# Small products of an RWKV-7 head pair: the odd head's results go to the other half of the rows, so that a group works in four quarters of TensorE

## The chip, the core and the metric

One core of a Trainium2 chip runs the whole program in one launch. The metric is the device time of one execution in microseconds (us). PE is TensorE, PEld its weight loads, DVE VectorE, ACT ScalarE, POOL GpSimd, SP SyncE (it issues most of the DMAs).

## What is computed

The reference is a trunk of two layers on 512 tokens of width 1024. Each layer is a half-step SwiGLU FFN, a mixing sub-layer and another FFN, each behind an RMSNorm with a shift, a scale and a gate from a condition vector. The mixing sub-layer projects the tokens to 20 tiles of 128 columns, and gives them to three kinds of heads: windowed attention (8 query heads), RWKV-7 time mixing (4 heads of 64) and a short convolution. The change is in the RWKV part only. What a head has to compute is this recurrence over the tokens:

```
def step(S, inp):
    r_t, w_t, k_t, v_t, kk_t, a_t = inp
    s_kk = einsum('bhvk,bhk->bhv', S, kk_t)
    S = S * w_t[:, :, None, :] - s_kk[..., None] * (kk_t * a_t)[:, :, None, :] + v_t[..., None] * k_t[:, :, None, :]
    return S, einsum('bhvk,bhk->bhv', S, r_t)
```

## The kernel before

The activations are kept transposed: 128 channels on the rows (partitions), 512 tokens along the columns. Large products are made in three passes of a split number format (`mm3`, lines 121 to 123: high by high, high by low, low by high), 128x128 weights by 512 columns, and each weight tile is split by ACT (`wH`, line 133) and DVE (`wL`, line 135) before use.

The recurrence is computed in chunks of 64 tokens. The function `rwkv(q)` does it for one pair of heads, q = 0 and q = 1; each layer calls it for both, so there are four calls. The two heads of a pair are e = 0 (channel rows 0 to 63) and e = 1 (rows 64 to 127), and the 8 chunks are numbered by block b (0 to 3) and half c (0 and 1): chunk n = 2b + c. In the tiles of a pair, chunk halves c lie on the rows, `rows[c]`, and e and b along the columns. The steps, with the names that the profile shows:

- `pairs` (L811) makes `B` (from `be`, the tile that was `a`) and `K` (from `ka`, the tile that was `iP`): products into two PSUM tiles `ps_c`, one for each e, then one masked copy for each by DVE (L814). The matrix to be inverted is `LT`, a part of `B`.
- The 16x16 blocks of its diagonal are inverted by DVE, after a detour by DRAM (`elim`, `inv`, L839 and L840). The result, `C`, becomes the tile `T` and by a transpose `TT` (L888, L889).
- `ps_xv` (L874): `K` times the values, copied by ACT to a half of `AX` (L875).
- Two levels that put the blocks together: `X` = mask of `LT` by `T` (products `ps_x`, DVE L902), `T` minus `TT` by `X` (products `ps_t`, L906, at level 0 only), and `TT` minus `X` by `TT` (products `ps_tt`, L909).
- `W` = minus `TT` by `AX` (products `ps_w2`, which the profile calls `ps_w`, L916; ACT L917, one copy for each e).
- `ps_gn` (L926 to L933), `ps_o` (L942 to L949), then the six serial steps over the chunks (`ps_s`, L954), `ps_ys`, the group norm (`ps_m`, `ps_v`, a reciprocal at L972, L973 and L974) and the gate (`ps_g`).

All of these are 64x64 or 64x128 products, 64 rows deep. Which quarter of TensorE's 128x128 array a product takes follows from where its operands' rows and its result's rows lie. In `ps_xv`, `ps_x`, `ps_t`, `ps_tt` and `ps_w2` the result stands on the same rows as the operands, so that only two of the four quarters are used:

```
def each(name, lhs, rhs):
    pt = psum([P, 2, NB, CH], name, R)
    for e in range(2):
        for b in range(NB):
            for c in range(2):
                mm(pt[rows[c], e, b], lhs[rows[c], e, b], rhs[rows[c], e, b], start=True, stop=True)
    return pt
```

In `ps_c`, `ps_gn` and `ps_o` the operands lie on the rows of one of c and e, the results on the rows of the other: four quarters. Each head pair has one PSUM tag (`R` is r0 or r1) with two buffers.

The order of the work is set in two stages. `rwkv` and `attention` are generators; each `yield` names a cost in us, and the loop at the end of `mix` puts steps of the projection (`products`, one step is three large products) between them, in proportion to that cost: RWKV_WORK and ATT_WORK are the sums of the yields, FILL_WORK the projection work there is to share out. After that a scheduler orders the instructions of each engine by what it expects to be ready, so that products of one group can be put between those of another. On the chip each engine then works off its list in order.

Of the kernel before, what the change touches and what calls it, by code (L numbers as in the profile page):

```python
# [12 lines left out]
ALU = mybir.AluOpType  # L13
# [4 lines left out]
P = 128  # L18
# [8 lines left out]
NB = T // P  # L27
CH = 64
# [3 lines left out]
PAD = 24  # L32
GAP = 448
GROUPS = ((0, 12), (12, 22))
RWKV_WORK, ATT_WORK, FILL_WORK = 29.8, 15.2, 129.6


def _columns(spec):
# [20 lines left out]
def trunk_kernel(ctx, tc, ins, out, layers=L, phases=("ffn1", "mix", "ffn2")):  # L59
    nc = tc.nc  # L60
# [14 lines left out]
    tt, stt, ts = nc.vector.tensor_tensor, nc.vector.scalar_tensor_tensor, nc.vector.tensor_scalar  # L75
    act, mm = nc.scalar.activation, nc.tensor.matmul
# [7 lines left out]
    def psum(shape, name, tag="x"):  # L84
        return ps.tile(shape, F32, name=name, tag=tag, bufs=2)

    def psmm(tags=("mm",)):
        turn[0] += 1
        return psum([P, T], "ps_mm", tags[turn[0] % len(tags)])
# [49 lines left out]
    rows = (slice(0, CH), slice(CH, P))  # L139
# [33 lines left out]
    def cst(name):  # L173
        a, b = CON[name]
        return con[:, a:b]

    def rep(name, n):
        a = cst(name)
        return a.unsqueeze(1).to_broadcast([P, n, a.shape[1]])

    def rep2(name, n):
        a = cst(name)
        return a.unsqueeze(1).unsqueeze(1).to_broadcast([P, 2, n, a.shape[1]])
# [100 lines left out]
    def load_w(src, n=KD, raw=None, pair=None, behind=None):  # L284

        w = raw or wp.tile([P, KD, P], F32, name="wraw", tag="wraw", bufs=2)
        wH, wL = pair or (wp.tile([P, KD, P], F32R, name=x, tag=x, bufs=4) for x in ("wH", "wL"))
        loads.append(nc.sync.dma_start(w[:, :n], src))
        split(wH[:, :n], wL[:, :n], w[:, :n], behind)
        return wH, wL  # L290
# [292 lines left out]
    def mix(l, hn, ss, mp, then, ready):  # L583
# [5 lines left out]
        def pair(name):  # L589
            pool = hnp[name in ("y4", "y5", "yr")]  # L590
            return tuple(pool.tile([P, T], F32R, name=name + n, tag="hn") for n in "HL")

        def S(q, name, shape=(P, T)):
            return mp.tile(list(shape), F32, name=f"{name}{q}", tag=f"s{q}", bufs=8)

        def U(q, name, shape):
            return mp.tile(shape, F32, name=f"{name}{q}", tag=f"u{q}", bufs=4)
# [147 lines left out]
        def rwkv(q):  # L745

            R = f"r{q}"
# [56 lines left out]
            def pairs(src, name):  # L804
                M = U(q, name, [P, 2, NB, 2, CH])
                pts = [psum([P, NB, 2, CH], "ps_c", R) for _ in range(2)]
                for b in range(NB):
                    for c in range(2):
                        n = 2 * b + c
                        for e in range(2):  # L810
                            mm(pts[e][rows[c], b], src[rows[e], n * CH : (n + 1) * CH], AR[rows[e], :, n], start=True, stop=True)  # L811
                msk = con[:, CON["su"][0] : CON["iu"][1]].unsqueeze(1).to_broadcast([P, NB, 2 * CH])
                for e in range(2):
                    tt(M[:, e].rearrange("p b a t -> p b (a t)"), pts[e].rearrange("p b a t -> p b (a t)"), msk, ALU.mult)  # L814
                yield 1.4
                return M

            B_ = yield from pairs(be, "B")
            LT = B_[:, :, :, 0]

# [6 lines left out]
            for c in range(2):  # L827
                for m in range(NM):
                    n = (c * NM + m) * 2 * NB
# [6 lines left out]
            for s in range(BASE - 1):  # L836
                n = BASE - 1 - s
# [10 lines left out]
            AX = U(q, "AX", [P, 2, NB, 2, CH])  # L848
# [7 lines left out]
            def tcopy(src, name):  # L856
                t = blocks(S(q, name))
                nc.scalar.copy(t, tmajor(src, "ps_" + name))
                return t

            def alphas():
                pt = tmajor(AR[:, 0].rearrange("p c t -> p (c t)"), "ps_ta")
                for e in range(2):
                    nc.scalar.copy(AX[:, e, :, 0], pt[:, :, rows[e]])


            K_ = yield from pairs(ka, "K")
            vN = tcopy(v_[q], "vN")
            yield 0.4
            px = psum([P, 2, NB, CH], "ps_xv", R)  # L870
            for e in range(2):
                for b in range(NB):
                    for c in range(2):
                        mm(px[rows[c], e, b], K_[rows[c], e, b, 0], vN[rows[c], b, rows[e]], start=True, stop=True)  # L874
            nc.scalar.copy(AX[:, :, :, 1], px)  # L875
            yield 1.3
            alphas()
            yield 0.4
            beN = tcopy(be, "beN")
# [4 lines left out]
            T_ = S(q, "T", (P, 2, NB, CH))  # L884
            TT = S(q, "TT", (P, 2, NB, CH))
# [3 lines left out]
            nc.vector.transpose(TT.rearrange("p e b t -> p (e b t)"), T_.rearrange("p e b t -> p (e b t)"))  # L889
            X = S(q, "X", (P, 2, NB, CH))  # L890

            def each(name, lhs, rhs):
                pt = psum([P, 2, NB, CH], name, R)
                for e in range(2):
                    for b in range(NB):
                        for c in range(2):
                            mm(pt[rows[c], e, b], lhs[rows[c], e, b], rhs[rows[c], e, b], start=True, stop=True)
                return pt

            for lev in range(2):  # L900
                px = each("ps_x", LT, T_)
                tt(X, px, rep2(f"lev{lev}", NB), ALU.mult)  # L902
                yield 1.3
                if lev == 0:
                    p1 = each("ps_t", TT, X)
                    tt(T_, T_, p1, ALU.subtract)  # L906
                    yield 1.3
                p2 = each("ps_tt", X, TT)
                tt(TT, TT, p2, ALU.subtract)  # L909
                yield 1.3  # L910
            Wn = AX.rearrange("p e b a t -> p e b (a t)")
            for e in range(2):
                pt = psum([P, NB, P], "ps_w2", R)
                for b in range(NB):
                    for c in range(2):
                        mm(pt[rows[c], b], TT[rows[c], e, b], Wn[rows[c], e, b], start=True, stop=True)  # L916
                nc.scalar.mul(Wn[:, e], pt, -1.0)  # L917
                yield 1.1

            GT = chunks(S(q, "GT"))  # L920
            N = chunks(S(q, "N"))
            pgs = [psum([P, 2, NB, CH], "ps_gn", R) for _ in range(2)]
            ce = [(c, e) for c in range(2) for e in range(2)]
            for b in range(NB):
                for c, e in ce:
                    mm(pgs[c][rows[e], 0, b], Wn[rows[c], e, b, :CH], beN[rows[c], b, rows[e]], start=True, stop=True)  # L926
# [13 lines left out]
            for b in range(NB):  # L940
# [4 lines left out]
                for c, e in ce:  # L945
                    mm(pos[c][rows[e], 1, b], vN[rows[c], b, rows[e]], K_[rows[c], e, b, 1], start=False, stop=True)
            for c, po in enumerate(pos):
# [3 lines left out]
            for c in range(1, NC - 1):  # L951
                pt = psum([P, CH], "ps_s", R)
# [4 lines left out]
            pt = psum([P, NC, CH], "ps_ys", R)  # L957
# [107 lines left out]

        prod = products()
        live, waiting = {}, {"rwkv0": lambda: rwkv(0), "rwkv1": lambda: rwkv(1), "att": attention}
        left, fill, credit = 2 * RWKV_WORK + ATT_WORK, FILL_WORK, 0.0
        more = True
# [28 lines left out]
        for q in range(2):  # L1098
            x = pair("yr")
# [3 lines left out]
        for n in range(2):  # L1103
            w = load_w(wo2[l, n], 6)
            for d in range(3):
                i = 3 * n + d
                pt = psmm(BANKS[1:3])
# [10 lines left out]
        for i, w, _ in got["last"]:  # L1118
            pt = psmm(BANKS[1:3])[:, : T // 2]
# [140 lines left out]
    for n, (l, p) in enumerate(seq):  # L1260
# [3 lines left out]
        if n + 1 < len(seq):  # L1264
            l1, p1 = seq[n + 1]
# [15 lines left out]
        else:  # L1281
            w, need = ("w1", (l, 7)) if p == "ffn1" else ("w2", (l + 1, 1))
# [88 lines left out]
```

## Time and profile before

| | us |
|---|---|
| median of 3 runs | 1867.47 (1863.78 to 1871.3) |
| the profiled execution, its time | 1866.04 |
| its span | 1864.0 |
| PE busy | 1828.7 (98%) |
| DVE busy | 1398.4 (75%) |
| ACT busy | 836.3 (45%) |

Engines' busy times overlap; PE's are partly modelled, since matmuls are pipelined. In the rows of the profile an fp32 product shows as two records. The groups of the change lie between 465 and 568 us in layer 0, and between 1378 and 1482 us in layer 1.

### The profile page before, as it was taken

The numbers are of one execution on the slowest core, as the hardware profiler recorded it, in microseconds if no ns is written. First come the engines' busy times: TensorE is split into PE (matmuls) and PEld (weight loads), VectorE is DVE, ScalarE is ACT, GpSimd is POOL, SyncE is SP. The second block draws the span as 40 slices with busy tenths as digits, with TensorE's granted clock in tenths as the row PEclk, the third lists the DMA queues.
The fourth block names the chain that finished last, engine by engine and source line by source line (L and its number), as shares of the span: only waits on it lengthen the run. The fifth ranks groups of instructions, "written<-read, shape, count | busy, mean of one in ns | idle before, by whom it ended". The sixth has DMA issues, their size and how long they took to land.

```text
span 1864.0 us, 33421 instructions
## 1 busy us (share of the span) xinstructions
PE 1828.7 (98%) x13664; PEld 1644.4 (88%) x13664; DVE 1398.4 (75%) x2202; ACT 836.3 (45%) x1272; POOL 130.9 (7%) x212
## 2 busy tenths in 40 slices
PE   8999999999999999999999999999999999999999
PEld 6889899986777999899999988999767788998998
DVE  7687677867986887777878786777589778874872
ACT  4443255346422555245345524544563335532551
POOL 0101110100000000110100020110000000100100
PEclk8999999999999999999999999999999999999999
DMA  7667876621122475886737688773212125775752
GB/s 307 225 185 234 263 197 202 221 83 46 58 55 72 136 195 176 296 223 195 246 112 197 171 272 228 192 229 114 101 56 59 53 68 161 209 227 139 203 144 68
DMA packets 104313, 308.24 MB, mean 165 GB/s; under 512 B 23392, under 2 KB 24416, under 8 KB 103136
## 3 DMA queue, kind: packets, MB, share of 16 engines
q1 hardware_dynamic: 75936, 203.34, 32.3%
q0 software_dynamic: 28224, 102.77, 21.7%
q8 instruction: 107, 1.75, 0.4%
q14 instruction: 46, 0.38, 0.1%
HBM read 302.66 MB, written 3.41 MB: 164 GB/s over the span
## 4 chain that ended last, share of the span: by engine, by line
PE 71%; DVE 13%; DMA 7%; issue 4%; ACT 4%; POOL 1%; SPq 0%; POOLq 0%; DVEq 0%; ACTq 0%
PE ps_mm L121 11%; PE ps_mm L122 10%; PE ps_mm L123 10%; PE ps_d L420 6%; PE ps_d L422 6%; PE ps_d L421 6%; PE ps_f L420 3%; PE ps_f L422 3%; PE ps_f L421 3%; DMA wada<-in_wadaT 2%; DVE wL L135 2%; PE ps_g L422 2%; PE ps_g L420 2%; PE ps_g L421 2%; ACT wH L133 1%
## 5 line engine op out<-in xcount | busy, mean ns | idle before, releaser
L133 ACT CAST wH<-wraw 128x1024 fp32r<-128x1024 f32 (+2 forms) x292 | 266.1, 918 | 434.7 <-PE ps_mm L122 190.2
L135 DVE TENSOR_TENSOR wL<-wraw,wH 128x1024 fp32r<-128x1024 f32 (+2 forms) x292 | 307.2, 1058 | 105.1 <-ACT wH L133 104.4
L123 PE MATMUL ps_mm<-actH,wL 128*128 128x512 f32 (+1 forms) x784 | 281.5, 359 | 2.8 <-DVE wL L135 2.8
L121 PE MATMUL ps_mm<-actH,wH 128*128 128x512 f32 (+1 forms) x784 | 281.6, 359 | 0.0
L122 PE MATMUL ps_mm<-actL,wH 128*128 128x512 f32 (+1 forms) x784 | 281.2, 359 | 0.0
L121 PE MATMUL ps_mm<-hnH,wH 128*128 128x512 f32 (+1 forms) x760 | 267.5, 359 | 5.7 <-ACT hnH L133 2.9
L122 PE MATMUL ps_mm<-hnL,wH 128*128 128x512 f32 (+1 forms) x760 | 266.5, 353 | 0.5
L123 PE MATMUL ps_mm<-hnH,wL 128*128 128x512 f32 (+1 forms) x760 | 266.4, 353 | 0.6 <-DVE wL L135 0.6
L420 PE MATMUL ps_d<-comH,wH 128*128 128x256 f32 x816 | 224.7, 275 | 0.3 <-ACT s L446 0.3
L421 PE MATMUL ps_d<-comL,wH 128*128 128x256 f32 x816 | 224.4, 275 | 0.0
L422 PE MATMUL ps_d<-comH,wL 128*128 128x256 f32 x816 | 224.4, 275 | 0.0
L192 DVE SCALAR_TENSOR_TENSOR wada<-wada,crep 128x1024 f32<-128x1024 f32 x140 | 167.7, 1219 | 48.8 <-DMA wada<-in_wadaT 48.2
L135 DVE TENSOR_TENSOR wL<-sum,wH 128x1024 fp32r<-128x1024 f32 x102 | 124.9, 1224 | 71.5 <-ACT wH L133 71.3
L123 PEld LDWEIGHTS ps_mm<-actH,wL 128*128 128x128 f32 x784 | 149.1, 190 | 20.3 <-DVE wL L135 3.6
L121 PEld LDWEIGHTS ps_mm<-hnH,wH 128*128 128x128 f32 x760 | 143.4, 191 | 24.9 <-issue 3.8
L121 PEld LDWEIGHTS ps_mm<-actH,wH 128*128 128x128 f32 x784 | 149.1, 190 | 16.8
L122 PEld LDWEIGHTS ps_mm<-actL,wH 128*128 128x128 f32 x784 | 149.0, 190 | 16.8
L123 PEld LDWEIGHTS ps_mm<-hnH,wL 128*128 128x128 f32 x760 | 145.5, 191 | 19.3 <-issue 4.3
L122 PEld LDWEIGHTS ps_mm<-hnL,wH 128*128 128x128 f32 x760 | 145.4, 192 | 17.2 <-DVE hnL L277 1.6
L420 PEld LDWEIGHTS ps_d<-comH,wH 128*128 128x128 f32 x816 | 156.7, 192 | 0.9 <-ACT s L446 0.9
L422 PEld LDWEIGHTS ps_d<-comH,wL 128*128 128x128 f32 x816 | 156.7, 192 | 0.0
L421 PEld LDWEIGHTS ps_d<-comL,wH 128*128 128x128 f32 x816 | 156.7, 192 | 0.0
(354 smaller groups left out, 3855.6 us busy)
## 6 DMA issues: line engine op xcount, KB each, us to landing
wada<-in_wadaT POOLq DMA_DIRECT2D x128, 512.0 KB, 4.8
wraw<-in_wmi SPq DMA_DIRECT2D x40, 512.0 KB
wraw<-in_w2p SPq DMA_DIRECT2D x36, 512.0 KB
wraw<-in_w1p SPq DMA_DIRECT2D x32, 512.0 KB
wraw<-in_w1o SPq DMA_DIRECT2D x32, 384.0 KB
wraw<-in_w2o SPq DMA_DIRECT2D x32, 384.0 KB
wraw<-in_w1i SPq DMA_DIRECT2D x20, 512.0 KB
wraw<-in_w1o SPq DMA_DIRECT2D x32, 320.0 KB
```

Source lines behind the costliest of these rows:

```text
L121: mm(acc, wH, xH, start=start, stop=False)
L122: mm(acc, wH, xL, start=False, stop=False)
L123: mm(acc, wL, xH, start=False, stop=stop)
L133: nc.scalar.copy(hi, src)
L135: return nc.vector.tensor_sub(lo, src, hi.bitcast(F32))
L192: stt(w, w, 1.0, crep, ALU.mult, ALU.mult, accum_out=out_)
L420: mm(acc, wH, xH, start=start and i + k == 0, stop=False, skip_group_check=True)
L421: mm(acc, wH, xL, start=False, stop=False, skip_group_check=True)
L422: mm(acc, wL, xH, start=False, stop=k == 3, skip_group_check=True)
```

## The change

The products of `ps_xv`, `each` and `ps_w2` put the odd head's (e = 1) results on the other half of the rows, `rows[c ^ e]`. The four combinations of e and c then lie in the four quarters of the array, and each group is issued in the order `corners`. For it each group gets two PSUM tiles, one for each e (`quarters`), and takes both buffers of its tag. The result is then read in three pieces (`gathered`): the even head as a whole, 128 rows, and the odd head as two halves of 64 rows which change places. At level 0 both products, the one for `T` and the one for `TT`, are put into one pair of tiles under the name `ps_t` (it was `ps_t` and `ps_tt`), and the yield between them goes. `W` is made for both heads at once. In `pairs`, `ps_gn` and `ps_o` the loops over e and c run backwards. The yields get other costs, and RWKV_WORK, their sum, falls from 29.8 to 25.7.

```diff
-RWKV_WORK, ATT_WORK, FILL_WORK = 29.8, 15.2, 129.6
+RWKV_WORK, ATT_WORK, FILL_WORK = 25.7, 15.2, 129.6
...
                     for c in range(2):
                         n = 2 * b + c
-                        for e in range(2):
+                        for e in (1, 0):
                             mm(pts[e][rows[c], b], src[rows[e], n * CH : (n + 1) * CH], AR[rows[e], :, n], start=True, stop=True)
...
+            corners = [(b, e, c) for b in range(NB) for e, c in ((1, 1), (1, 0), (0, 1), (0, 0))]
+
+            def quarters(name, n=1, w=CH):
+                return [psum([P, n, NB, w], name, R) for _ in range(2)]
+
+            def gathered(pts, j):
+                return [(slice(0, P), 0, pts[0][:, j])] + [(rows[c], 1, pts[1][rows[1 - c], j]) for c in range(2)]
...
-            px = psum([P, 2, NB, CH], "ps_xv", R)
-            for e in range(2):
-                for b in range(NB):
-                    for c in range(2):
-                        mm(px[rows[c], e, b], K_[rows[c], e, b, 0], vN[rows[c], b, rows[e]], start=True, stop=True)
-            nc.scalar.copy(AX[:, :, :, 1], px)
-            yield 1.3
+            pts = quarters("ps_xv")
+            for b, e, c in corners:
+                mm(pts[e][rows[c ^ e], 0, b], K_[rows[c], e, b, 0], vN[rows[c], b, rows[e]], start=True, stop=True)
+            for r, e, x in gathered(pts, 0):
+                nc.scalar.copy(AX[r, e, :, 1], x)
+            yield 0.8
...
+            def each(pts, j, lhs, rhs):
+                for b, e, c in corners:
+                    mm(pts[e][rows[c ^ e], j, b], lhs[rows[c], e, b], rhs[rows[c], e, b], start=True, stop=True)
 
             for lev in range(2):
-                px = each("ps_x", LT, T_)
-                tt(X, px, rep2(f"lev{lev}", NB), ALU.mult)
-                yield 1.3
+                pts = quarters("ps_x")
+                each(pts, 0, LT, T_)
+                for r, e, x in gathered(pts, 0):
+                    tt(X[r, e], x, rep(f"lev{lev}", NB)[r], ALU.mult)
+                yield 0.8
+                pts = quarters("ps_t", 2 - lev)
                 if lev == 0:
-                    p1 = each("ps_t", TT, X)
-                    tt(T_, T_, p1, ALU.subtract)
-                    yield 1.3
-                p2 = each("ps_tt", X, TT)
-                tt(TT, TT, p2, ALU.subtract)
-                yield 1.3
+                    each(pts, 1, TT, X)
+                each(pts, 0, X, TT)
+                for j, to in ((1, T_), (0, TT))[lev:]:
+                    for r, e, x in gathered(pts, j):
+                        tt(to[r, e], to[r, e], x, ALU.subtract)
+                yield 1.4 - 0.6 * lev
...
-            for e in range(2):
-                pt = psum([P, NB, P], "ps_w2", R)
-                for b in range(NB):
-                    for c in range(2):
-                        mm(pt[rows[c], b], TT[rows[c], e, b], Wn[rows[c], e, b], start=True, stop=True)
-                nc.scalar.mul(Wn[:, e], pt, -1.0)
-                yield 1.1
+            pts = quarters("ps_w2", 1, P)
+            for b, e, c in corners:
+                mm(pts[e][rows[c ^ e], 0, b], TT[rows[c], e, b], Wn[rows[c], e, b], start=True, stop=True)
+            for r, e, x in gathered(pts, 0):
+                nc.scalar.mul(Wn[r, e], x, -1.0)
+            yield 1.3
...
-            ce = [(c, e) for c in range(2) for e in range(2)]
+            ce = [(c, e) for c in (1, 0) for e in (1, 0)]
```

More of the change, by code (lines that the diff above doesn't have):

```diff
@@ L890, in rwkv @@
             X = S(q, "X", (P, 2, NB, CH))
-            def each(name, lhs, rhs):
-                pt = psum([P, 2, NB, CH], name, R)
-                for e in range(2):
-                    for b in range(NB):
-                        for c in range(2):
-                            mm(pt[rows[c], e, b], lhs[rows[c], e, b], rhs[rows[c], e, b], start=True, stop=True)
-                return pt
-            for lev in range(2):
-                px = each("ps_x", LT, T_)
-                tt(X, px, rep2(f"lev{lev}", NB), ALU.mult)
-                yield 1.3
-                if lev == 0:
-                    p1 = each("ps_t", TT, X)
-                    tt(T_, T_, p1, ALU.subtract)
-                    yield 1.3
-                p2 = each("ps_tt", X, TT)
-                tt(TT, TT, p2, ALU.subtract)
-                yield 1.3
@@ L911, in rwkv @@
-            Wn = AX.rearrange("p e b a t -> p e b (a t)")
-            for e in range(2):
-                pt = psum([P, NB, P], "ps_w2", R)
-                for b in range(NB):
-                    for c in range(2):
-                        mm(pt[rows[c], b], TT[rows[c], e, b], Wn[rows[c], e, b], start=True, stop=True)
-                nc.scalar.mul(Wn[:, e], pt, -1.0)
-                yield 1.1
+            def each(pts, j, lhs, rhs):
+                for b, e, c in corners:
+                    mm(pts[e][rows[c ^ e], j, b], lhs[rows[c], e, b], rhs[rows[c], e, b], start=True, stop=True)
```

## The prediction

> **What bounds the kernel now.** The page's head comes first.
>
> ```profile
> span 1864.0 us, 33421 instructions
> PE 1828.7 (98%) x13664; PEld 1644.4 (88%) x13664; DVE 1398.4 (75%) x2202; ACT 836.3 (45%) x1272; POOL 130.9 (7%) x212
> ```
>
> TensorE (PE) is busy for 98% of the span, so work taken off it can shorten the run one for one, but only where it does not then stand and wait. The share is a mean, so I read the stage of the change by windows (columns: length, then busy time of PE, its weight loads, VectorE = DVE, ScalarE = ACT, POOL). This is layer 0; layer 1's mixing repeats the same order.
>
> ```profile
> 500.00:520.00 20.00, 19.51 (x183) 15.80 (x184) 20.00 (x32) 3.58 (x5) 0.43 (x2) 1.00 0.33 96
> 520.00:540.00 20.00, 19.81 (x423) 16.12 (x419) 13.76 (x48) 6.12 (x12) 0.00 (x0) 1.00 0.19 48
> 540.00:560.00 20.00, 20.00 (x258) 15.35 (x259) 17.59 (x26) 6.37 (x10) 0.00 (x0) 1.00 0.15 42
> ```
>
> In the 60 us in which both pairs of RWKV heads run their inverse, PE lacks 0.68 us of being full, but DVE has 51.35 of 60 us, and all 20.00 in the first window. The change takes from PE and gives to DVE: the question is whether DVE has room at the places where PE waits for it. Next the groups of instructions that change.
>
> ```profile
> L897 PE MATMUL ps_x<-T,B 64*64 64x64 f32 x256 | 9.2, 221 | 0.0
> L897 PE MATMUL ps_tt<-TT,X 64*64 64x64 f32 x256 | 9.0, 220 | 0.0
> L916 PE MATMUL ps_w<-AX,TT 64*64 64x128 f32 x128 | 8.3, 274 | 0.0
> L902 DVE TENSOR_TENSOR X<-ps_x,con 128x512 f32<-128x512 f32 x8 | 5.5, 684 | 2.1 <-PE ps_x L897 2.1
> ```
>
> A group of 16 small products is 32 records (256 over 8 executions), each 64x64; ps_t and ps_xv are half as many (they run once per call, not at both levels).
>
> **What the products save.** The rate now, and the rate of a group that already uses four quarters, from start to start in the timeline:
>
> ```profile
> 519.30 1.15 PE L897 MATMUL ps_t<-X,TT 64*64 64x64 f32 x32
> 520.28 1.10 PE L897 MATMUL ps_tt<-TT,X 64*64 64x64 f32 x32
> ...
> 562.81 1.09 PE L916 MATMUL ps_w<-AX,TT 64*64 64x128 f32 x16
> 563.83 0.48 PE L121 MATMUL ps_mm<-y3H,wH 128*128 128x512 f32 x1
> ...
> 565.73 0.30 PE L926 MATMUL ps_gn<-beN,AX 64*64 64x64 f32 x8
> 566.08 0.30 PE L926 MATMUL ps_gn<-beN,AX 64*64 64x64 f32 x8
> ```
>
> Two quarters: 32 records in 0.98 us, 30.6 ns each. Four (ps_gn): 24 records from one L926 to the next, 0.35 us, 14.6 ns each. So a 32-record group saves 32 x 16.0 ns = 0.51 us; the 64x128 products of ps_w take 1.02 us for 16, about 2.0 for a head pair, and save 0.9 (half, less the entry). If all seven groups of a call gained, that were 6 x 0.51 + 0.9 = 4.0 us, and 16 over four calls.
>
> They do not all gain. Four quarters run only while the instruction order alternates between the two PSUM tiles, and in the changed program's order it often doesn't, because the second tile is still being read: the first head pair's ps_xv and both level-1 ps_x stand as 8 on one tile, then 8 on the other (nothing saved), the level-1 products as runs of 5 to 7 (I take 0.1 each). Full gain: level-0 ps_x 0.51 and its two products 1.02, ps_w 0.9, per head pair: 2.43, two make 4.9. The second ps_xv, in pieces of 4, 4, 3, 5, I give 0.35. The reversed orders of (c, e) let two groups alternate that did not: the second pair's B products (below, 1.43 us for 32 records; four-wide half of ps_w's rate, 0.98) 0.45, and the first pair's ps_o, which now needs 2.28 where its twin needs 1.63 (window on that tile): all but its first 8 products alternate, 0.5.
>
> ```profile
> 511.69 1.50 PE L811 MATMUL ps_c<-AR,a 64*64 64x128 f32 x32
> 513.12 0.48 PE L123 MATMUL ps_mm<-hnH,wL 128*128 128x512 f32 x1
> ...
> 531.30:534.00 2.70, 2.28 (x96) 2.16 (x96) 0.00 (x0) 0.00 (x0) 1.00 0.03 6
> 570.90:573.00 2.10, 1.63 (x96) 1.49 (x96) 0.37 (x2) 0.00 (x0) 1.00 0.23 39
> ```
>
> Sum per layer 4.9 + 0.2 + 0.35 + 0.45 + 0.5 = 6.4 us, in two layers **12.8 us**: that is the ceiling.
>
> [...] These rows show two records of ps_x, which has one PSUM bank, done in 0.22 us, the time of a single one, so its two row halves write one bank together.
>
> ```profile
> 517.21 0.22 PE L897 MATMUL ps_x<-T,B 64*64 64x64 f32 x2
> ```
>
> [...]
>
> **What the evictions cost.** One instruction of 128x512 becomes one of 128x256 and two of 64x256, since the odd head's halves change places. The trace has no 64x256; the nearest is 128x256 (ps_gn's), and fewer rows should not take longer.
>
> ```profile
> 530.54 0.41 DVE L932 TENSOR_TENSOR GT<-ps_gn,con 128x256 f32<-128x256 f32 x1
> 530.87 0.41 DVE L933 TENSOR_TENSOR N<-ps_gn,pc 128x256 f32<-128x256 f32 x1
> ```
>
> 0.41 alone, 0.33 from start to start in a row. Three in a row are ready after 1.07 us against 0.67: +0.4 each, five a call (X and TT twice, T once): 2.0 us of DVE, 8 us in all; with gaps between them up to 0.55 each (3 x 0.41 - 0.68). ACT's pieces (ps_xv, ps_w) cost at most three instead of two full ones; ACT is busy 6 of 20 us there, and I charge them only within the waits below.
>
> **First head pair: where DVE is full.**
>
> ```profile
> 517.38 1.17 DVE L135 TENSOR_TENSOR wL<-wraw,wH 128x1024 fp32r<-128x1024 f32 x1
> 518.49 0.67 DVE L902 TENSOR_TENSOR X<-ps_x,con 128x512 f32<-128x512 f32 x1
> 519.09 1.26 DVE L814 TENSOR_TENSOR K<-ps_c,con 128x512 f32<-128x512 f32 x2
> 520.28 0.93 DVE L135 TENSOR_TENSOR wL<-wraw,wH 128x768 fp32r<-128x768 f32 x1
> 521.15 0.67 DVE L906 TENSOR_TENSOR T<-T,ps_t 128x512 f32<-128x512 f32 x1
> ...
> 521.89 1.01 PEld L897 LDWEIGHTS ps_x<-T,B 64*64 64x64 f32 x32 [0.17 <-DVE T L906]
> ```
>
> ```profile
> 518.34 0.38 PE L123 MATMUL ps_mm<-hnH,wL 128*128 128x512 f32 x1
> 518.99 0.38 PE L123 MATMUL ps_mm<-hnH,wL 128*128 128x512 f32 x1
> ```
>
> A step of the projection (three products) takes 0.65 us, from L123 to L123. DVE runs its five lines without a gap, and PE waits 0.17 us for T. The order on DVE stays, so T comes 0.4 (X) + 0.4 (T) later: about 522.6. PE has 0.45 + 0.51 + 1.02 = 1.98 us less to do, but the new order puts 8.0 steps of projection before level-1 ps_x where 6.0 stood (1.3 us more) and 4 of ps_xv (0.12). It gets there at 521.72 - 1.98 + 1.42 = 521.16 and waits 1.45 us. Gain so far: 1.42 of work done ahead, 0.71 later: 0.7. From there to ps_gn, 0.9 (ps_w) and 0.35 (ps_xv) less about 0.55 of waits (level 1's pieces, ACT's third) leave 0.7. With ps_o's 0.5: **+1.9 us**.
>
> **Second head pair: behind the reciprocal.**
>
> ```profile
> 545.96 1.02 PE L610 MATMUL ps_v<-gnsq,con 128*128 128x512 f32 x2
> 548.10 3.35 DVE L972 RECIPROCAL gnrs<-gnrs 128x512 f32<-128x512 f32 x1
> 551.36 0.63 DVE L906 TENSOR_TENSOR T<-T,ps_t 128x512 f32<-128x512 f32 x1
> 551.90 0.74 DVE L973 SCALAR_TENSOR_TENSOR y<-y,par,gnrs 128x512 f32<-128x512 f32 x1
> 552.14 1.15 PE L897 MATMUL ps_x<-T,B 64*64 64x64 f32 x32
> 556.65 1.15 PE L897 MATMUL ps_tt<-TT,X 64*64 64x64 f32 x32
> ```
>
> Now T follows the reciprocal directly, and ps_x starts 0.7 us after the reciprocal's end. In the new order DVE has T, y, T, y, T there: 0.33 + 0.66 + 0.33 + 0.66 + 0.41 = 2.4 us until T is whole, 1.7 more. PE has 4.0 steps there (2.6 us, before 3.3) and 1.0 us less of products; it waits about 2 us. Behind it level-1 ps_x and the TT products stand with no step between them, where 5.0 stood: another wait of 1.3 to 1.8 for X's pieces. Against 2.5 us saved, and the steps that do come out earlier, I make this **-0.3 us**.
>
> Sum: 1.9 - 0.3 = 1.6 a layer, **3.2 us** in two. The yields' smaller numbers move projection steps only; PE's total of them stays. The profiled execution took 1866.04 us (span 1864.0), so 1862.8 after; the median of the runs, 1867.47, lies 1.43 above it, so **1864.3 us**.
>
> **The rivals.** *The whole saving comes through*: the scheduler's waits are not real because DVE's weight splits slip instead. For it: DVE is busy only 13.76 of 20 us in the second window. Against: the first window's 20.00. It gives 1867.47 - 12.8 = 1854.7.
>
> *Slower, DVE sets the end*: PE gains only where it wasn't waiting (B products 0.45, ps_w twice 1.8, ps_o 0.5: 2.75 a layer) and waits in full at T (1.45), at the pieces of level 1 (0.55), behind the reciprocal (2.7, if y's operations are all ahead of PE) and at the second X (1.8): 6.5. That is 3.7 a layer, 7.4 in all: 1874.9. It decides from the point where PE reaches the second level-1 ps_x over 2 us before T is whole.
>
> [...]
>
> **How the numbers follow.** About 0.5% (9.3 us) is what a measurement can tell from no change. Forecast 0.60, its own range 1858 to 1871; whole saving 0.20; slower 0.15; no wider 0.05. Beyond 1858.1: 0.18 of the whole saving's 0.20 and 0.04 of the forecast, faster 0.22. Above 1876.8: half of the slower rival and 0.02 of the others, slower 0.10. The rest, 0.68, is no change. The range takes in the whole saving and most of the slower rival: 1854 to 1873.
>
> **What would show it.** Right: level-0 ps_x in about 0.5 us for 32 records, ps_w in 1.0; three DVE pieces 0.33 apart; PE idle for DVE T ahead of level-1 ps_x by about 1.4 us in the first pair and 2 in the second. The forecast is wrong if these waits stay under 0.5 (then the whole saving), if the second pair's wait passes 2.7, or if level-0 ps_x still takes 0.98.

## The result, and the profile after

| | before | after |
|---|---|---|
| median, us (11 runs each) | 1867.48 (1861.65 to 1877.23) | 1876.05 (1873.93 to 1882.88) |
| ratio to before | | 1.0048, 95% interval [1.0032, 1.0063] |
| the profiled execution, us (span) | 1866.04 (1864.0) | 1875.55 (1873.5) |

The change makes the kernel slower by 0.48%, where 1864.3 us and no change were forecast, and the time lies above the stated range of 1854 to 1873. Ratios, here and below, are taken over all runs of a comparison and not from the two medians. The head of the page:

```profile
span 1873.5 us, 33485 instructions
PE 1820.0 (97%) x13664; PEld 1634.3 (87%) x13664; DVE 1410.7 (75%) x2242; ACT 840.5 (45%) x1284; POOL 131.2 (7%) x212
```

PE is busy 8.7 us less than before and the span is 9.5 us longer: PE stands for 18 us more. DVE has 12.3 us more to do, with 40 instructions more. The windows of layer 0 show where (columns as in the prediction; the number after the counts of POOL is the granted TensorE clock):

```profile
500.00:520.00 20.00, 17.55 (x231) 13.65 (x231) 19.82 (x35) 2.47 (x3) 0.42 (x2) 1.00 0.33 86
520.00:540.00 20.00, 16.81 (x365) 12.78 (x361) 13.12 (x50) 6.63 (x14) 0.00 (x0) 1.00 0.17 47
540.00:560.00 20.00, 16.83 (x230) 12.51 (x230) 18.79 (x32) 5.98 (x10) 0.00 (x0) 0.90 0.09 22
560.00:580.00 20.00, 20.00 (x294) 15.98 (x293) 12.43 (x23) 5.97 (x10) 0.00 (x0) 0.92 0.23 75
```

In the first 60 us PE is busy for 51.19, where it was for 59.32, and behind 540 us the clock is no longer 1.00. From the first `ps_q` of a layer's mixing to the first `ps_ss` behind it (start times of PE in the traces) layer 0 took 218.0 us and takes 223.3, layer 1 took 217.8 and takes 223.5. These **mixing stages** hold the loss, 5.3 + 5.7 = 11.0 us; the rest of the span moves by a few us from profile to profile, so below the stages are compared.

What PE waits for between 500 and 572 us, first before, then after (columns: total us, times, longest):

```profile
PE ps_bo L610 <- DVE bonus L788: 0.3, 1, 0.3
PE ps_c L811 <- DVE B L814: 0.2, 1, 0.2
PE ps_s L954 <- ACT y L949: 0.2, 1, 0.2
```

```profile
PE ps_x L902 <- DVE TT L916: 4.0, 2, 3.1
PE ps_o L948 <- DVE N L939: 2.5, 1, 2.5
PE ps_t L902 <- DVE X L908: 0.9, 2, 0.7
...
PE ps_gn L932 <- ACT AX L923: 0.4, 1, 0.4
```

The groups of `X` and `ps_x` (before, `X` was 8 instructions, 5.5 us, and `ps_x` never idle):

```profile
L908 DVE TENSOR_TENSOR X<-ps_x,con 64x256 f32<-64x256 f32 (+1 forms) x24 | 10.1, 421 | 0.8 <-PE ps_x L902 0.3
...
L902 PE MATMUL ps_x<-T,B 64*64 64x64 f32 x256 | 9.4, 230 | 9.5 <-DVE TT L916 8.0 <-DVE T L896 1.1
```

Twenty-four pieces of 421 ns; the same table with its shapes kept apart gives 422 ns to the sixteen of 64x256 alone.

```profile
L908 DVE TENSOR_TENSOR X<-ps_x,con 64x256 f32<-64x256 f32 x16 | 6.8, 422 | 0.4
```

Half the rows of a 128x256 piece took as long as all of them: the eight whole pieces of `X` have a mean of 418 ns. The first head pair in the timeline (rows of PE, DVE and ACT):

```profile
512.24 0.72 PE L902 MATMUL ps_x<-T,B 64*64 64x64 f32 x32
512.83 1.09 PE L811 MATMUL ps_c<-AR,iP 64*64 64x128 f32 x22
514.44 1.29 DVE L908 TENSOR_TENSOR X<-ps_x,con 128x256 f32<-128x256 f32 x3
515.87 0.69 PE L902 MATMUL ps_t<-X,TT 64*64 64x64 f32 x32 [0.67 <-DVE X L908]
516.36 0.68 PE L902 MATMUL ps_t<-TT,X 64*64 64x64 f32 x32
517.95 1.29 DVE L916 TENSOR_TENSOR T<-T,ps_t 64x256 f32<-64x256 f32 x3
519.25 1.32 DVE L916 TENSOR_TENSOR TT<-TT,ps_t 128x256 f32<-128x256 f32 x3
519.72 0.62 PE L902 MATMUL ps_x<-T,B 64*64 64x64 f32 x14 [0.96 <-DVE TT L916]
...
525.38 1.80 ACT L923 ACTIVATE AX<-ps_w 64x512 f32<-64x512 f32 x3
527.23 0.34 PE L932 MATMUL ps_gn<-beN,AX 64*64 64x64 f32 x8 [0.42 <-ACT AX L923]
...
531.50 0.18 DVE L839 TENSOR_TENSOR elim<-G,inv 64x28 f32<-64x28 f32 x1
531.61 0.74 DVE L938 TENSOR_TENSOR GT<-ps_gn,con 128x256 f32<-128x256 f32 x2
532.83 0.33 PE L948 MATMUL ps_o<-B,AX 64*64 64x64 f32 x4 [2.47 <-DVE N L939]
```

The products are as quick as forecast (`ps_x` 0.59 us to the next start, `ps_t` 0.49), but three pieces take DVE 1.29 to 1.32 us, and PE waits behind them. Ahead of `ps_o` it waits for another reason too: `ps_gn` is done at 528.9, but DVE works off the second pair's `elim` and `inv` until 531.6 before it turns to `GT` and `N`. The second pair:

```profile
548.69 3.35 DVE L978 RECIPROCAL gnrs<-gnrs 128x512 f32<-128x512 f32 x1
551.96 0.36 DVE L916 TENSOR_TENSOR T<-T,ps_t 128x256 f32<-128x256 f32 x1
552.28 0.38 PE L121 MATMUL ps_mm<-y4H,wH 128*128 128x512 f32 x1
...
554.12 0.42 DVE L916 TENSOR_TENSOR T<-T,ps_t 64x256 f32<-64x256 f32 x1
554.55 0.69 DVE L987 TENSOR_TENSOR y<-y,ps_g 128x512 f32<-128x512 f32 x1
555.15 1.31 DVE L916 TENSOR_TENSOR TT<-TT,ps_t 128x256 f32<-128x256 f32 x3
555.72 1.93 PE L902 MATMUL ps_x<-T,B 64*64 64x64 f32 x32 [3.05 <-DVE TT L916]
557.51 1.78 PE L902 MATMUL ps_t<-TT,X 64*64 64x64 f32 x32
559.22 0.79 PE L121 MATMUL ps_mm<-y4H,wH 128*128 128x512 f32 x1
559.81 0.63 PE L122 MATMUL ps_mm<-y4L,wH 128*128 128x512 f32 x1
560.23 0.63 PE L123 MATMUL ps_mm<-y4H,wL 128*128 128x512 f32 x1
```

`T` is whole at 554.54, yet `ps_x` starts only when the first piece of `TT` has been read too, 3.05 us after PE's last product: both products of level 0 lie in one pair of tiles, and `ps_x` needs their buffers. And then PE is slow: its large products start 0.42 us apart, where the prediction's rows have three in 0.65.

### The profile page after: what moved, and what is told of

Same layout as the page of the kernel before. It is cut to its first block, busy times and chain, and to the rows that moved or that the text cites. A ratio compares the mean times of both kernels' runs of the same rounds, so it can differ in the third digit from the quotient of the medians.

```text
span 1873.5 us, 33485 instructions
## 1 busy us (share of the span) xinstructions
PE 1820.0 (97%) x13664; PEld 1634.3 (87%) x13664; DVE 1410.7 (75%) x2242; ACT 840.5 (45%) x1284; POOL 131.2 (7%) x212
## 3 DMA queue, kind: packets, MB, share of 16 engines
HBM read 302.66 MB, written 3.41 MB: 163 GB/s over the span
## 4 chain that ended last, share of the span: by engine, by line
PE 67%; DVE 15%; DMA 9%; issue 4%; ACT 4%; POOL 1%; SPq 1%; DVEq 0%; ACTq 0%; POOLq 0%
PE ps_mm L121 10%; PE ps_mm L122 10%; PE ps_mm L123 10%; PE ps_d L420 6%; PE ps_d L421 6%; PE ps_d L422 6%; PE ps_f L421 3%; PE ps_f L420 3%; PE ps_f L422 3%; DMA wada<-in_wadaT 3%; DVE wL L135 2%; PE ps_g L422 2%; PE ps_g L421 2%; PE ps_g L420 2%; ACT wH L133 1%
```

## The experiments

Theory **P**: the loss is the DVE time of the three pieces, which PE waits for. Rivals: the order or width of the products, ACT's pieces, the yields, the two PSUM buffers, the group norm's reciprocal, the clock. Every edit has the scheduler order the instructions anew, so a comparison holds that too; what counts is whether many edits agree.

**Pieces without quarters, quarters without the third piece, the reversed loops alone.** e1 leaves the odd head's halves exchanged and reads each group in two whole pieces:

```diff
-return [(slice(0, P), 0, pts[0][:, j])] + [(rows[c], 1, pts[1][rows[1 - c], j]) for c in range(2)]
+return [(slice(0, P), e, pts[e][:, j]) for e in range(2)]
```

> The change, but the odd head's tile is read in one piece of 128 rows, without changing its halves back (so from ps_xv on the odd head is computed on swapped halves: that part of the computation is changed). Two pieces of 128x256 stand for one of 128x512. Theory A, the third piece and the crossing of rows make the evictions long (0.43 us from piece to piece where ps_gn's take 0.33) and PE waits for them: about 8 us faster than the changed kernel, 1866 to 1869, the longest wait ahead of ps_x under 2.5 us. Theory B, the new spacing of the projection steps (yields) lets PE reach DVE's results too early: stays at 1873 to 1877.

e2 takes the four quarters away and keeps three pieces:

```diff
-mm(pts[e][rows[c ^ e], j, b], ...
+mm(pts[e][rows[c], j, b], ...
-... [(rows[c], 1, pts[1][rows[1 - c], j]) for c in range(2)]
+... [(rows[c], 1, pts[1][rows[c], j]) for c in range(2)]
```

> Products on two quarters as before (each group in two tiles, one for each head), evictions in the change's three pieces, its yields. What the evictions and the order cost without the products' gain. Theory A: as slow as the changed kernel or slower by up to 8 us, since the waits are set by DVE and the slower products only fill them: 1876 to 1884. Theory B: about the same time as the changed kernel plus the whole 12.8 us that the products lost: 1886 to 1890.

e4 is the kernel before with the loops of `pairs`, `ps_gn` and `ps_o` backwards:

```diff
-ce = [(c, e) for c in range(2) for e in range(2)]
+ce = [(c, e) for c in (1, 0) for e in (1, 0)]
```

> The kernel before with only the loops over c and e run backwards in the products of B and K, ps_gn and ps_o. Both theories: not the cause; within 2 us of before (the first pair's ps_o and the second pair's B products may lose 0.5 us each a layer).

Measured: e1 1865.0 us, ratio to before 0.9977 [0.9966, 0.9988]; e2 1879.99, 1.0058 [1.004, 1.0077]; e4 1869.06, 0.9997 [0.9983, 1.0011]. The timelines of e1 and of e2:

```profile
515.16 0.73 DVE L908 TENSOR_TENSOR X<-ps_x,con 128x256 f32<-128x256 f32 x2
```

```profile
517.80 1.19 DVE L908 TENSOR_TENSOR X<-ps_x,con 128x256 f32<-128x256 f32 x3
```

One piece of 64 rows more cost 0.46 us (1.19 against 0.73) even where no result changes rows. Without it the four quarters bring a gain (in e1, which computes something else for the odd head); with it and without the quarters all of the loss is there. For P, against the order of the loops. e2 also bears on the clock: in its layer 0 the granted clock is 1.00 from 500 to 580 us, and the mixing stage is still 221.7 us long, 3.7 more than before.

**Whose pieces?** e8 has four quarters and three pieces only in ACT's groups (`ps_xv`, `ps_w`), e15 only in DVE's (`ps_x`, `ps_t`):

```diff
 e8, against the kernel after:
-pts = quarters("ps_x")
-each(pts, 0, LT, T_)
+px = each("ps_x", LT, T_)
+tt(X, px, rep2(f"lev{lev}", NB), ALU.mult)
 ...  (ps_t and ps_tt likewise; RWKV_WORK 28.4)
```

```diff
 e15, against the kernel after:
-pts = quarters("ps_w2", 1, P)
+pt = psum([P, NB, P], "ps_w2", R)
 ...  (one per head; ps_xv in one tile; RWKV_WORK 27.1)
```

> Only the two groups that ScalarE evicts (ps_xv, ps_w) and the reversed loops take the change; level 0 and 1 (ps_x, ps_t, ps_tt), which DVE evicts, stay as before. All theories: DVE has nothing more to do, so the saving of 0.9 us a call for ps_w shows: 1863 to 1867. If the change's loss came from the ACT groups instead, above 1870.

> The changed kernel with ps_xv and ps_w as before (two quarters, one tile or one per head), so only the groups that DVE evicts have four quarters and three pieces; the counterpart of e8, where only the groups of ACT had them (1.0012). Theory (DVE's pieces are the loss): all of the loss or nearly, 1873-1878. Rival (the loss needs both parts, ACT's third piece delaying AX and W): 1868-1871.

e8: 1870.57 us, 1.0012 [0.9996, 1.0027]. e15: 1878.94, 1.0052 [1.0034, 1.0071]. DVE's groups alone make a loss as large as the whole change. e8 is a miss: the gain that was expected of `ps_w` did not come, and its median lies just above the 1870 that was to speak against ACT's groups. Its interval takes in no change and a loss of up to 0.27%, so a small share of theirs is not excluded. In layer 0 of its trace PE waits 1.5 us for `N` ahead of `ps_o` and 1.6 us for the second pair's first `T`, with no third piece on DVE. So waits of this kind come without those pieces too, and P does not cover all of them.

**Is it DVE's time?** e11 takes work from DVE and leaves products and pieces as they are. The level's mask is multiplied into `LT` ahead of time by POOL, so `X` is a plain copy, which ACT makes in the same three pieces. (`T` is block diagonal where it meets `LT`, so masking before the product gives the same `X`.) e12 does it to the kernel before, e16 to e15.

```diff
+X = S(q, "X", (P, 2, NB, CH))
+for i, to in ((0, X), (1, LT)):
+    for e in range(2):
+        nc.gpsimd.tensor_tensor(to[:, e], LT[:, e], rep(f"lev{i}", NB), ALU.mult)
+LM = (X, LT)
...
-each(pts, 0, LT, T_)
+each(pts, 0, LM[lev], T_)
-tt(X[r, e], x, rep(f"lev{lev}", NB)[r], ALU.mult)
+nc.scalar.copy(X[r, e], x)
 e12: each("ps_x", LM[lev], T_) and nc.scalar.copy(X, px)
```

> The changed kernel, with the mask of each level multiplied into the triangular factor ahead of time on POOL, so that X is a plain copy, and all twelve X pieces of a layer are written by ACT instead of DVE. DVE is rid of 4 x 1.2 to 1.3 us a layer. Theory (DVE's pieces set the waits): the waits at the first pair's level-1 ps_x (0.96) and the second pair's (3.2, of which X's pieces are not the first part) shrink, the mixing stages fall by 2 to 5 us each from 223.3 and 223.5, time 1866-1872. Rival (the chain of pieces is as long on ACT, 3 x 0.4 us, and DVE's room is not what lacks): stages and time within 1.5 us of the changed kernel, 1874-1878.

> The kernel before with the same masks put ahead on POOL and X copied by ACT in one piece. DVE is rid of 4 x 0.67 = 2.7 us a layer. Theory (in the first pair DVE is full already, 20.00 of 20 us, and PE waits little): a gain of 0 to 3 us, 1864-1868, ratio 0.998-1.000. Rival (DVE bounds the kernel before as it does the changed one): 4 us and more faster, ratio below 0.998. If ACT's copy comes later than DVE's did, 1869-1871.

> e15 with X on ACT as in e11. Theory (DVE's pieces are the loss and ACT's groups bring nothing): as e11, 1863-1867. If ACT, which now has X, is better without third pieces of AX and W: below 1864. Rival (as e15): X on ACT no help, 1873 or more.

e11: 1864.99 us, 0.999 [0.9975, 1.0004], 11 us less than the changed kernel; mixing stages 218.7 and 217.7. e16: 1869.91, 1.0013 [0.9999, 1.0027], against 1.0052 of e15. e12: 1869.36, 1.0015 [0.9999, 1.0031]. The three longest of PE's waits in e11 (500 to 572 us), and POOL's new group:

```profile
PE ps_x L905 <- DVE TT L919: 2.0, 2, 1.4
PE ps_o L951 <- DVE N L942: 1.1, 1, 1.1
PE ps_gn L935 <- ACT AX L926: 0.8, 1, 0.8
```

```profile
L846 POOL TENSOR_TENSOR X<-B,con 128x256 f32<-128x256 f32 x8 | 6.5, 809 | 271.5 <-DVE B L814 271.5
```

The waits named in the changed kernel are the ones that shrink (4.0 to 2.0, 2.5 to 1.1), though `TT` and `N` themselves have not changed: DVE gets to them earlier. Before the change the same relief brings nothing: PE was not waiting there, and in e12 it waits 1.1 us for ACT instead. So DVE's room became the limit with the change. e16 was to equal e11 and came out 5 us above it; that ACT loaded with X would gain by whole pieces of `W` (its second guess) did not show either, and no run explains the difference.

**Other suspects, in the changed kernel.** e3 has the old yields, e5 gives level-1 `ps_x` and `ps_o` PSUM buffers of another tag, e6 records the first pair's reciprocal behind the second pair's level-0 `T` and `TT`, e7 does both, e9 adds unused products that were meant to keep PE busy in the two long waits.

```diff
 e3
-RWKV_WORK = 25.7; yields 0.8 / 0.8 / 1.4 - 0.6 * lev / 1.3
+RWKV_WORK = 29.8; yields 1.3 / 1.3 / 2.6 - 1.3 * lev / 2.2
 e5
-pts = quarters("ps_x")
+pts = quarters("ps_x", tag="x" if lev else R)
-pos = [psum([P, 2, NB, CH], "ps_o", R) for _ in range(2)]
+pos = [psum([P, 2, NB, CH], "ps_o", "x") for _ in range(2)]
 e6
+while q == 0 and "T1" not in done:
+    yield 0.0
 nc.vector.reciprocal(rs, rs)
 e9
+if q == 1 and lev == 1:
+    waste(10)          # ones by ones, 128x512, into a PSUM tile of tag x
+if q == 0:
+    waste(6)           # ahead of ps_o
```

> The change with the yields of before (1.3, 1.3, 2.6 or 1.3, 2.2; sum 29.8): more projection steps between the groups. Theory A: little, within 3 us of the changed kernel's 1876. Theory B: the waits ahead of ps_x and ps_o fall below 1 us each, 1863 to 1869.

> The change, but level 1's ps_x and ps_o take their two PSUM tiles from the tag x, which attention no longer needs there, so that they need not wait until the last piece of the group before has been read. Theory A1, the pieces' own DVE time is all: ps_x still waits for T, ps_o has no data to wait for; 1 to 3 us faster than the change, 1873 to 1876. Theory A2, the buffers: the waits of 2.6 us ahead of ps_o and of 1.1 us ahead of the first pair's level-1 ps_x go, and 1 us of the second pair's; about 8 us faster than the change, 1866 to 1870.

> The change, but the first pair's reciprocal, and the operations on y behind it, are recorded after the second pair's level-0 T. Theory A3, DVE's order: the wait of 3.2 us ahead of the second pair's level-1 ps_x falls below 1 us, and the halved clock behind it (6.8 us in layer 0, 3.4 us in layer 1, worth up to 5 us) goes: 1865 to 1870. Theories A1 and A2: T comes earlier, but TT's pieces and the buffers keep ps_x waiting: 1872 to 1877.

> Both: the tag x and the reciprocal behind T. If A2 and A3 each own a part, 1861 to 1867, below the kernel before; if the pieces' DVE time (A1) is the bound, not below 1868.

> Ten 128x512 products that nobody uses stand ahead of the second pair's level-1 ps_x and six ahead of the first pair's ps_o, at the two longest waits of the changed kernel (3.2 and 2.6 us); at 0.22 us each they take 2.2 and 1.3 us. Theory (beside the waits, the clock granted at half behind them costs up to 3.4 us in layer 0 and 1.7 us in layer 1): the products lie in the waits, no stretch at half clock is left, the mixing stages come down from 223.3 and 223.5 to about 220 and 222, the time to 1871-1873. Rival (DVE sets the end, PE at half clock only waits less): stages and time stay, 1875-1877. If the waits have moved elsewhere: up to 2 x 3.5 us more, 1883.

| | us | ratio to before | mixing stages, us |
|---|---|---|---|
| e3 | 1880.04 | 1.0052 [1.0032, 1.0072] | 224.3, 223.7 |
| e5 | 1880.04 | 1.0065 [1.0039, 1.009] | 224.5, 226.3 |
| e6 | 1877.65 | 1.0046 [1.003, 1.0062] | 222.9, 224.6 |
| e7 | 1881.41 | 1.006 [1.0039, 1.0081] | 223.0, 222.3 |
| e9 | 1878.12 | 1.0058 [1.0037, 1.008] | 224.5, 224.3 |

None repairs anything: the waits move. In e5, slower than either of its theories had it, PE waits for the pieces of `X` instead (ps_t, 3.5 us in three waits) and for `St` (3.2). The extra products of e9 were a miss: in layer 0 they ran at 489.6 us and from 549.2 to 551.6, while the waits ahead of `ps_x` came at 516.9 and 560.6 (1.8 us each). The granted clock still fell, to a mean of 0.93, 0.90 and 0.91 in three of the four windows of 20 us from 500 to 580 us, so e9 says nothing on the clock's share.

**A version with two pieces.** In e13 the odd head's `X`, `TT` and `AX` stay on the other rows, so that `AX`, `X`, `T` and `W` are read in two whole pieces. `TT` has to stay on its own rows, so `ps_tt` goes back to two quarters and one 128x512 piece; the first `TT` and the alphas (the other half of `AX`) are written in three pieces. e10 was the same with RWKV_WORK left at 25.7, though its yields add up to 26.9; e14 is e13 with `X` on ACT.

```diff
+return [(slice(0, P), e, pts[e][:, j]) for e in range(2)]
...
+nc.vector.transpose(TT[:, 0] ..., T_[:, 0] ...)
+for c in range(2):
+    nc.vector.transpose(TT[rows[1 - c], 1] ..., T_[rows[c], 1] ...)
...
+if lev == 0:
+    pts = quarters("ps_t")
+    each(pts, 0, TT, X)
+    for r, e, x in gathered(pts, 0):
+        tt(T_[r, e], T_[r, e], x, ALU.subtract)
+    yield 0.8
+p2 = inplace("ps_tt", X, TT)      # out on rows[c]
+tt(TT, TT, p2, ALU.subtract)
+yield 1.3
 e10: RWKV_WORK = 25.7; e13, e14: RWKV_WORK = 26.9
```

> The odd head's X, TT and AX stay on the other half of the rows, so the values' share, X, T and W are evicted in two whole pieces of 128x256 and TT in one of 128x512; ps_tt goes back to two quarters, and the alphas and the first TT are written in three pieces. Theory (the third, 64-row piece is what costs): the loss of the changed kernel is gone; against the kernel with two pieces everywhere (ratio 0.9977) ps_tt gives back about 1 us per pair and layer at most, so 1865-1869, ratio 0.998-1.001. Rival (two tiles and their order cost by themselves, whatever the pieces): 1873 or more, ratio 1.003 or more.

> As e10, with the sum of the pair's yields put right (RWKV_WORK 26.9 for 25.7; in e10 the second pair ended too late and PE stood 3.9 us per layer for its last y). Theory (the third, 64-row piece is what costs): without that wait 1865-1871, ratio 0.999-1.002, and the mixing stages near 218. Rival (two tiles per group cost by their order, whatever the pieces): e10 less 7.8, 1880, ratio 1.007.

> e13 and X copied by ACT in two pieces, with the level masks multiplied ahead on POOL. Theory (DVE's pieces set the waits): at least as good as e11 (1865.0), 1860-1866, ratio 0.996-0.999. Rival (X on ACT gains only because it takes a third piece off DVE, of which there is none here): the same as e13.

e10: 1887.93 us, 1.0112 [1.0088, 1.0136]. e13: **1865.74 us, 0.9979 [0.9966, 0.9993]**, mixing stages 217.1 and 217.0. e14: 1869.02, 1.0011 [0.9992, 1.0031]. PE's waits from 600 us on in e10, and the three longest of 500 to 572 us in e13:

```profile
PE ps_mm L121 <- DVE y L997: 3.7, 1, 3.7
```

```profile
PE ps_s L970 <- ACT y L965: 1.2, 1, 1.2
PE ps_t L905 <- DVE X L917: 1.1, 1, 1.1
PE ps_tt L910 <- DVE X L917: 0.7, 2, 0.6
```

e10, expected at 1865 to 1869, was a miss. Its budget let the projection run out before the second pair was done: PE stood 3.7 us for its last `y` in each layer, and the waits within the mixing came out worse as well; one number in the planner is worth 22 us here. With it put right, the version is faster than both kernels, than the one before by 0.07 to 0.34%. X on ACT does not help it: e14 was to be at least as good as e11 and is not. That there was no third piece left to take off DVE is the likely reason, not a shown one.

All kernels together: those in which DVE reads `X`, `T` and `TT` in three pieces (after, e2, e3, e5, e6, e7, e9, e15) lie at 1.0046 to 1.0065; those in which it reads fewer, e10 apart, at 0.9977 to 1.0015. So P stands for the cause of the loss: the third pieces on DVE. How the lost time divides between their own length, the order of DVE's work that goes with them and the clock, the runs tell in part only.

## Why the prediction was wrong, by its own steps

In short: per layer the prediction had 6.4 us saved by the products, 4.8 lost again to waits, and 1.6 gained. By PE's busy time in the mixing stages, with the products' saving taken from e1, 5.8 and 5.5 us were saved in the two layers, the waits took 8.1 and 9.6 more than before, and the slower clock an estimated 2.9 and 1.5: 5.3 and 5.7 us lost.

- **What the products save, 6.4 us a layer: nearly right.** 32 records of level-0 `ps_x` take 0.59 us, of `ps_t` 0.49, `ps_w` 1.03. e1 has the change's products and a granted clock of 1.00 from 500 to 580 us: in its mixing stages PE is busy for 207.9 and 208.0 us, where it was for 213.6 and 213.4 before. That is 5.8 and 5.5 us less. The 0.95 for the reversed loops shows in e4, whose mixing stages are 217.1 us both, 0.9 and 0.7 shorter than before, though its time of 1869.06 does not tell. Where the products stand on one tile at a time nothing is saved, as forecast: the records of the first pair's level-1 `ps_x`, 16 on one tile and then 16 on the other, start in pairs 0.058 us apart, 29 ns each; those of its level 0, in alternation, start in fours 0.058 us apart.
- **Both row halves in one tile: no hindrance.** Each tile of `ps_x` now takes the products of both halves of the operands' rows, and the group takes 0.59 us, not 0.98, and the first of `ps_t` 0.49. These are 18 and 15 ns a record, near the 14.6 of `ps_gn`. So the groups ran wider, against the 0.05 for no wider.
- **What the evictions cost, +0.4 each: this step failed.** The spacing of 0.33 us came from whole 128x256 pieces, and the text said that fewer rows should not take longer. They take as long, 422 ns, and in a row of three they stand 0.43 apart instead of 0.33; the prediction's own upper bound, +0.55 each, would have been nearer. A group is ready 1.29 to 1.32 us after its start, where the prediction had 1.07: +0.6 to 0.65, and DVE's busy time rose by 12.3 us, not 8.
- **First pair, +1.9: failed, but not at the wait that it named.** Level-1 `ps_x` waited 0.96 us, less than the 1.45 forecast, though behind another 0.67 at `ps_t`. What was missed lies later. `ps_gn` waits 0.42 us for `AX`, since a 64x512 piece of ACT lasts as long as a whole one (0.59 us against 0.60 for 128x512 before). And `ps_o`, booked at +0.5, waits 2.47 us for `N`: DVE's own order puts the second pair's elimination ahead of `GT` and `N`, which the prediction had not followed.
- **Second pair, -0.3: failed.** `T` was whole 2.5 us after the reciprocal's end (2.4 forecast). But the prediction let `ps_x` start with `T`; both products of level 0 share one pair of tiles, which take both buffers, and these are free only when `TT` has been read as well. So the gate was `TT`'s first piece, behind `y`: 3.05 us for "about 2", past the 2.7 at which the prediction called itself wrong. The mechanism priced under *slower, DVE sets the end* came true at nearly its price (1874.9 against 1876.05), though its point of decision did not describe it: PE was done 1.9 us before `T` was whole, not over 2, and the end was set by `TT`. That the price fits is partly luck: its sum has neither the wait at `ps_o` nor the clock. And the range, said to take in most of this rival, ended at 1873, below the rival's own price.
- **Not in the sum at all: the clock.** Below.

## What to carry to other kernels

Before a product is spread over more of the array, count what its reader has to do: two quarters more saved PE 0.4 to 0.5 us a group, and one 64-row piece more cost DVE 0.46 to 0.6, on an engine that had no room at that place. A result that has landed on other rows was better left there, with its next operands moved to match (e13), than put back by half-height copies. Where a planner shares out work by stated costs, they have to add up again after every edit: a sum short by 1.2 per head pair cost more than the change itself.

## What the runs showed of the hardware

- Half the rows saved DVE no time: a 64x256 piece of `X` took 422 ns and a 128x256 piece 418 (means in after; 414 is the median of the sixteen of 128x256 in e1). Half the columns did: 128x512 took 684 ns before.
- Two pieces of DVE did not always follow each other equally closely. Two whole 128x256 pieces start 0.33 us apart, before the first has ended (`GT` and `N` before), and two take 0.73 together (`X` in e1). In after, every direct step to or from a 64-row piece within a group of `X`, `T` or `TT` takes 0.41 to 0.46, and the next piece starts 13 to 32 ns after the last has ended. In e2, where no result changes rows, four of the first pair's groups in layer 0 took 1.18 to 1.20 and the fifth, its level-1 `X`, 1.33. What sets the step from piece to piece, no run shows.
- The granted clock fell to 0.50 after the long waits: in layer 0 for 6.83 us, from about 556.2 us on, in layer 1 for 3.41 us, from about 1481.2 us on, by the trace's record of the clock; the rows from 559.22 us on show it. Before, it is 1.00 in the mixing of both layers; in e1 and e13 it is 1.00 from 500 to 580 us. By half of these lengths, an estimate, the slower clock costs up to 3.4 + 1.7 = 5.1 us of the 11.0. PE's busy time says 2.9 + 1.5 = 4.4: 210.8 and 209.5 us in the mixing stages of after, against 207.9 and 208.0 in e1 with the same products (an estimate, since the products' order differs a little). In the 3.41 us before the clock fell, PE stood for 2.9 us in layer 0 and for 1.9 in layer 1; what made it fall, no run shows. If it was the waits, they cost more than their length. No run here has the waits without the slower clock in both layers, so its share stays an estimate.
